# Gate weights loaded together, x copied out of PSUM before it is split, and a weight subtraction moved to VectorE

## The chip, the cores and the metric

The kernel runs on one core of one Trainium2 chip. The metric is the device time of one execution in microseconds (us); lower is better. The time before is a median of 3 runs.

## What is computed

One encoder layer over 1024 tokens of width 1024, all in float32:

```python
xn = rms_norm(x, norm_g)
qa, ka, va, za, qb, kb, vb, zb = split(xn @ w_in)     # eight blocks of 512 columns
ya = diff_attention(rms_norm(qa), rms_norm(ka), va, lam, t5_bias)   # 4 heads, two softmax maps each
ya = rms_norm(ya, subln_g) * (1 - lam_init) * silu(za)
yb = neighbourhood_attention(rms_norm(qb), rms_norm(kb), vb, na_rpb) * silu(zb)  # 8 heads, 8 x 16 window
x = x + concat(ya, yb) @ w_out
x = x + sigmoid(x @ w_ple_gate) * (p @ w_ple_proj)
```

## The kernel before

Every float32 operand of a product is split into a rounded high part and the remaining low part. A product is three matmuls (high by high, high by low, low by high). ScalarE (ACT) makes the high part with a copy, VectorE (DVE) the low part with a subtraction.

**The stages.** Up to 25 us the first row tiles of `x` are normalised, transposed and split. From 25 to about 303 us the input projection runs. It takes the six column blocks kb, vb, qb, qa, ka, va as three pairs, and works each pair with seven products of 512 x 512 quarters (P1 to P7, Winograd's scheme) in place of eight. P2 of all three pairs comes first, then P1, P6, P7, P4, P5, P3 of each pair. Each product is two steps on TensorE (PE) of 24 matmuls (L232 to L234), some 5.5 us each, 42 steps (`NS`) in all. Step h = 0 works the row tiles 0 and 1 of its quarter, step h = 1 the tiles 2 and 3. Neighbourhood attention follows to about 480 us, then differential attention to about 720 us, then the output projection and the last gate.

**The order.** Each engine executes its instructions in the order in which the program is written. Between the matmuls of step i the program places `hooks[i]`: pieces of other work with a number of their own. The tiles come from pools whose buffers go round: the weights `wraw` (L97 loads, 128x512) and many small tiles share pool b2 (11 buffers), wider tiles use b4 (8), and 4 PSUM buffers serve transposes and small products. All ordinary loads and stores leave by one queue of SyncE (SP), in program order. Two engines that read the same PSUM tile are put in order one after the other.

**x_trans(t)** (L360): PE transposes a row tile into two PSUM tiles `xtp` (L368). For tiles 0 to 3 `split` makes the quarters A11 and A12 (high `xh`, L357 on ACT; low `xl`, L358 on DVE), and ACT copies both PSUM tiles in float32 to `xf` (L373), which later sums need. `x_trans(2)`, a small product (`ple_mm(4)`, L312, result `pp` at L314), `x_trans(3)` and `x_norm(4)` stand in this order in the hook of step 0, between its two halves.

**The weights of P6** (`RIGHT`): its right factor is a sum of three quarters. `w_load` loads two raw quarters r and o per 128 rows. `w_sum1` subtracts r - o on GpSimd (POOL, L179). `w_sum2` adds the result to the quarter b11 that P1 left (L191, DVE), one chunk of 128x512 at a time. Two chunks are treated per step, for pair 0 in the iterations i = 5 and i = 6. In the same iterations `x_splits` gives POOL one more sum, `xsum` (L395), and DVE the low parts of S1, S2 and S3.

**The gates.** The columns zb and za (512 each) are taken as eight gate columns of 128. `z_load` loads a column's raw weights `zraw`, `z_split` makes the halves `zw` (L555 on ACT, L558 on DVE), and the product `zps` (L580 to L582) fills PE's gaps in neighbourhood attention. For the za columns the finished halves `zth` are stored to DRAM (`uad`). With `small=True` a column comes in two loads of 256 KB into b2 tiles, without it in one load of 512 KB into a b4 tile. The first column is loaded small in the hook of step NS - 4, the second whole in that of step NS - 1.

**Neighbourhood attention** works 32 units. A unit has scores on PE (`nsp`, L645), bias and maximum on DVE (L660), exponentials on ACT (L665), the division on DVE (L671, L673), transposes on PE (`ntp`, L683), their copy on ACT (`PT`, L685), the product with the values on PE (`npv`, L698) and the gate on DVE (`nay`, L708). Its operands K, Q, R and Vw come over the SP queue.

Of the kernel before, what the change touches and what calls it, by code (L numbers as in the profile page):

```python
# [11 lines left out]
OP = mybir.AluOpType  # L12
# [3 lines left out]
P = 128  # L16
# [8 lines left out]
COL = dict(qa=0, ka=512, va=1024, za=1536, qb=2048, kb=2560, vb=3072, zb=3584)  # L25
# [15 lines left out]
def layer_kernel(ctx, tc, x, p, ngr, w_in, w_out, gains, lamv, t5p, rpbp, w_gate, w_ple,  # L41
# [13 lines left out]
    def T8(shape, dt=F32, n="t8"):  # L55
        return sb.tile(shape, dt, name=nm(n), tag="b8", bufs=16)

    def T4(shape, dt=F32, n="t4"):
        return sb.tile(shape, dt, name=nm(n), tag="b4", bufs=8)

    def TA(shape, dt=F32, n="ta"):
        return sb.tile(shape, dt, name=nm(n), tag="a4", bufs=6)

    def T2(shape, dt=F32, n="t2"):
        return sb.tile(shape, dt, name=nm(n), tag="b2", bufs=NB2)
# [17 lines left out]
    def PS(shape, n="ps"):  # L83
        return psp.tile(shape, F32, name=nm(n), tag="ps", bufs=4)
# [11 lines left out]
    def ld(o, i):  # L96
        return nc.sync.dma_start(raw(o), raw(i))  # L97

    def st(o, i):
        return nc.sync.dma_start(raw(o), raw(i))  # L100
# [7 lines left out]
    V = nc.vector  # L108
# [48 lines left out]
    raws = {}  # L157
# [14 lines left out]
    def w_sum1(j):  # L172

        if j >= len(chunks):
            return
        pi, n, k = chunks[j]
        if n == "P6":
            r, o = raws[j]
            G.tensor_tensor(r, r, o, op=OP.subtract)  # L179
        elif n == "P4":  # L180
            r = raws[j][0]
            G.tensor_tensor(r, r, tk["t2", k], op=OP.subtract)

    def w_sum2(j):

        if j >= len(chunks):
            return
        pi, n, k = chunks[j]
        if n == "P6":
            r, t = raws[j][0], tk["b11", k]  # L190
            V.tensor_tensor(t, t, r, op=OP.add)  # L191
            tk["t3", k], tk["t2", k] = r, t
            raws[j] = t
        elif n == "P7":
            raws[j] = tk.pop(("t3", k))
        elif n == "P5":
            r, t = raws[j][0], tk.pop(("t2", k))
            V.tensor_tensor(t, r, t, op=OP.subtract)
            tk["b22", k] = r
            raws[j] = t  # L200
        elif n == "P3":
            raws[j] = tk.pop(("b22", k))
        else:
            raws[j] = raws[j][0]
# [150 lines left out]
    def split(n, ts, src, low):  # L355
        h, l = XA[n]
        act(h[:, :, ts], src, AF.Copy)  # L357
        low.tensor_tensor(l[:, :, ts], src, h.bitcast(F32)[:, :, ts], op=OP.subtract)  # L358

    def x_trans(t):  # L360
        hat = xhats.pop(t)
        u = t % 4
        ts = slice(u * P, u * P + P)
        pt = [PS([P, 4, P], "xtp") for _ in range(2)]
        for b in range(2):
            for k in range(4):
                kc = 4 * b + k
                nc.tensor.transpose(pt[b][:, k], hat[:, kc * P:(kc + 1) * P], idn)  # L368
        if t < 4:
            split("A11", ts, pt[0], V)  # L370
            split("A12", ts, pt[1], V)
            for b in range(2):
                act(xf[b][:, u], pt[b], AF.Copy)  # L373
            return
        s, d = xsum[0][:, u], xsum[1][:, u]
        a21 = TA([P, 4, P], n="a21s")
        act(a21, pt[0], AF.Copy)
        pst.append(lambda: st(a21d[:, :, ts], a21))
        V.tensor_tensor(s, pt[1], a21, op=OP.add)
        split("A22", ts, pt[1], V)  # L380
        V.tensor_tensor(d, xf[0][:, u], pt[0], op=OP.subtract)
        split("S1", ts, s, V)
        V.tensor_tensor(s, s, xf[0][:, u], op=OP.subtract)

    xsum = []
    xf = []
# [14 lines left out]
    def x_reload():  # L401
        r = T8([P, 4, 512], n="a21r")
        ld(r, a21d)
        XA["a21r"] = r

    def x_resplit():
        r = XA["a21r"]
        XA["A21"] = (T8([P, 4, 512], F32R, n="xh"), T8([P, 4, 512], F32R, n="xl"))
        h, l = XA["A21"]
        for k in range(2):  # L410
            ks = slice(2 * k, 2 * k + 2)
            act(h[:, ks], r[:, ks], AF.Copy)
            zl.append(lambda ks=ks: V.tensor_tensor(l[:, ks], r[:, ks], h.bitcast(F32)[:, ks], op=OP.subtract))
# [124 lines left out]
    def z_load(col, small=False):  # L538
        src = w_in[:, col:col + P].rearrange("(k q) d -> q k d", q=P)
        if small:  # L540
            r = [T2([P, 4, P], n="zraw") for _ in range(2)]
            for i in range(2):
                ld(r[i], src[:, 4 * i:4 * i + 4])
            zraw[col] = lambda a, b: r[a // 4][:, a % 4:(b - 1) % 4 + 1]
            return
        r = T4([P, 8, P], n="zraw")
        ld(r, src)
        zraw[col] = lambda a, b: r[:, a:b]

    def z_split(col, k0=0, k1=8):  # L550
        r = zraw[col]
        if k0 == 0:
            zw[col] = T8([P, 2, 8, P], F32R, n="zw")
        w = zw[col]
        act(w[:, 0, k0:k1], r(k0, k1), AF.Copy)  # L555

        def low():
            V.tensor_tensor(w[:, 1, k0:k1], r(k0, k1), w.bitcast(F32)[:, 0, k0:k1], op=OP.subtract)  # L558

        zl.append(low)  # L560
# [4 lines left out]
    def z_low():  # L565
        while zl:
            zl.pop(0)()
# [37 lines left out]
    def load_k(pr):  # L605
        k1 = T8([P, 2, S], F32R, n="K1")
        h, l = qkd["kb"]
        for (dst, s) in ((k1[0:64], h), (k1[64:128], l), (K2[pr % 2][0:64], h)):
            ld(dst, s[pr].rearrange("(h d) s -> d h s", h=2))
        kb[pr] = k1  # L610

    def load_q(pr, R):
        q1 = T4([P, 2, 512], F32R, n="Q1")
        h, l = qkd["qb"]
        for (dst, s) in ((q1[0:64], h), (q1[64:128], h), (Q2[R][0:64], l)):
            ld(dst, s[pr, :, R * 512:(R + 1) * 512].rearrange("(h d) s -> d h s", h=2))
        qb[pr, R] = q1

    def load_r(pr):
        r = []  # L620
        for h in range(2):
            t = TA([P, 752], n="R")
            ld(t, ap_of(rpbp, (2 * pr + h) * 23 * 48 + 1, [[48, 8], [1, 16], [1, 752]]))
            r.append(t)
        Rt[pr] = r

    def load_v(pr, R, j):
        w = WID[j]
        v = T15([P, 3, P], n="Vw")
        for m in range(3):  # L630
            r0 = 4 * R + 4 * m
            ld(v[0:4 * w, m], ap_of(vbd, (r0 * 64 + COL0[j]) * 512 + pr * P, [[64 * 512, 4], [512, w], [1, P]]))
        Vw[pr, R, j] = v
# [94 lines left out]
    def na_consts_q():  # L728
        for R in range(2):
            q = T4([P, 2, 512], F32R, n="Q2")  # L730
            for h in range(2):
                cast(q[64:128, h], onehot[:, R * 512:(R + 1) * 512])
            Q2.append(q)

    def load_r0():
        t = T8([P, 2, 752], n="R0")
        Rt[0] = [t[:, h] for h in range(2)]
        for h in range(2):
            ld(t[:, h], ap_of(rpbp, h * 23 * 48 + 1, [[48, 8], [1, 16], [1, 752]]))
# [90 lines left out]
    def pre(i):  # L830
        if i >= len(units):
            return
        pr, R, j = units[i]
        if j == 0:
            if R == 0:
                load_q(pr, 1)
            elif pr + 1 < 4:
                load_q(pr + 1, 0)
        if (R, j) == (0, 2) and pr + 1 < 4:
            load_k(pr + 1)  # L840
        if (R, j) == (1, 2) and pr + 1 < 4:
            load_r(pr + 1)
        if i + 2 < len(units):
            load_v(*units[i + 2])
# [22 lines left out]
    for j in range(6):  # L867
        w_sum2(j)
# [6 lines left out]
    ple_t(3)  # L875
    w_split(1)
    x_trans(0)
    ple_mm(2)
    ple_st()
# [54 lines left out]
    def s7():  # L934
# [3 lines left out]
    NS = len(steps)  # L938
# [8 lines left out]
        31: lambda: u_load(31),  # L947
        NS - 7: lambda: (na_consts_k(), load_k(0)),
        NS - 5: lambda: (load_r0(), x_reload()),
        NS - 4: lambda: z_load(COL["zb"], True),  # L950
        NS - 2: lambda: (na_consts_q(), load_q(0, 0), load_v(0, 0, 0), load_v(0, 0, 1), z_split(COL["zb"], 0, 4),
                         z_split(COL["zb"], 4, 8), z_low()),
        NS - 1: lambda: (pre(0), x_resplit(), z_load(COL["zb"] + P)),
        NS: na_consts_k,
    }
    lam_in = []
    normed = []
    for i in range(len(steps) + 2):
        w_sum1(LA - 2 + 2 * i)
        w_sum1(LA - 1 + 2 * i)  # L960
        if i < len(steps):
            step_mm(i, 0, 2)
# [4 lines left out]
        if got:  # L967
            n, t0, c = got
            if n[0] == "v":
                v_evac(n, t0, c)  # L970
            else:
                normed.append((n, t0, c, qk_norm1(c)[1]))
        w_sum2(LA - 2 + 2 * i)
        w_sum2(LA - 1 + 2 * i)
        w_load(LA + 2 * i)
        w_split(4 + 2 * i)
# [480 lines left out]
```

## Time and profile before

| | |
|---|---|
| median of 3 runs | 836.67 us (835.38 to 838.21) |
| the profiled execution | 838.91 us, of which 837.1 us span |
| mean granted TensorE clock | 0.978 |
| busy | PE 94%, PEld 78%, DVE 61%, ACT 52%, POOL 32% |

The span is what the trace covers; 1.81 us lie around it. PE is TensorE's matmuls and PEld its weight loads, which run beside them. A name such as `xl<-xtp` reads "tile xl written from tile xtp". "Idle before" is the time in which the engine did nothing ahead of that instruction, followed by what ended it.

### The profile page before, as it was taken

The numbers are of one execution on the slowest core, as the hardware profiler recorded it, in microseconds if no ns is written. First come the engines' busy times: TensorE is split into PE (matmuls) and PEld (weight loads), VectorE is DVE, ScalarE is ACT, GpSimd is POOL, SyncE is SP. The second block draws the span as 40 slices with busy tenths as digits, with TensorE's granted clock in tenths as the row PEclk, the third lists the DMA queues.
The fourth block names the chain that finished last, engine by engine and source line by source line (L and its number), as shares of the span: only waits on it lengthen the run. The fifth ranks groups of instructions, "written<-read, shape, count | busy, mean of one in ns | idle before, by whom it ended". The sixth has DMA issues, their size and how long they took to land.

```text
span 837.1 us, 12190 instructions
## 1 busy us (share of the span) xinstructions
PE 783.7 (94%) x4242; PEld 649.8 (78%) x4242; DVE 511.8 (61%) x986; ACT 437.6 (52%) x814; POOL 266.2 (32%) x267
## 2 busy tenths in 40 slices
PE   7899799999989994998979998999999999999997
PEld 6678588888878883776767776888888877888886
DVE  4557795685997662653635658777777752732332
ACT  5665355255435532554545569889888861411120
POOL 1003443261565400110101124677776761200000
PEclk9999899999999997999999999999999999999999
DMA  8655461945788999576666768757686437223222
GB/s 330 272 175 172 170 186 59 325 128 132 173 280 241 217 298 235 140 178 180 200 168 183 175 206 225 216 154 209 163 236 174 144 124 268 85 76 101 83 94 88
DMA packets 118525, 151.94 MB, mean 181 GB/s; under 512 B 23832, under 2 KB 76728, under 8 KB 118336
## 3 DMA queue, kind: packets, MB, share of 16 engines
q1 hardware_dynamic: 116672, 145.39, 59.0%
q0 software_dynamic: 1792, 5.77, 2.2%
q8 instruction: 34, 0.56, 0.3%
q14 instruction: 27, 0.22, 0.1%
HBM read 104.96 MB, written 46.17 MB: 181 GB/s over the span
## 4 chain that ended last, share of the span: by engine, by line
PE 71%; DVE 8%; DMA 7%; ACT 5%; issue 4%; SPq 2%; POOL 2%; ACTq 0%; DVEq 0%; POOLq 0%
PE ips L232 7%; PE ips L234 7%; PE ips L233 7%; PE dsp L1064 6%; PE gps L1259 3%; PE gps L1257 3%; PE gps L1258 3%; PE dtp L1106 3%; DMA uad<-zth 3%; PE ntp L683 3%; PE pps L312 2%; PE zps L580 2%; PE zps L582 2%; PE zps L581 2%; DMA Vw<-vb 2%
## 5 line engine op out<-in xcount | busy, mean ns | idle before, releaser
L232 PE MATMUL ips<-w,xh 128*128 128x512 f32 x336 | 135.0, 402 | 5.6 <-DVE C L258 4.1
L234 PE MATMUL ips<-w,xl 128*128 128x512 f32 x336 | 132.5, 394 | 0.0
L233 PE MATMUL ips<-w,xh 128*128 128x512 f32 x336 | 132.3, 394 | 0.0
L1089 POOL TENSOR_TENSOR s<-s,s 128x1024 f32<-128x1024 f32 x32 | 77.0, 2408 | 56.9 <-ACT s L1088 52.3
L431 POOL TENSOR_TENSOR qrs<-qms,nhalf 128x16 f32<-128x16 f32 x16 | 51.7, 3233 | 91.5 <-DVE qms L429 91.5
L1074 DVE CUSTOM_DVE_ANT_0 s<-dsp,T 128x1024 f32<-128x1024 f32 x64 | 77.7, 1215 | 2.5 <-PE dsp L1064 2.5
L232 PEld LDWEIGHTS ips<-w,xh 128*128 128x128 f32 x336 | 64.2, 191 | 19.3 <-issue 4.8
L1076 ACT ACTIVATE s<-s,dm 128x1024 f32<-128x1024 f32 x64 | 73.4, 1146 | 4.6 <-DVE dm L1074 4.5
L234 PEld LDWEIGHTS ips<-w,xl 128*128 128x128 f32 x336 | 63.9, 190 | 13.9
L233 PEld LDWEIGHTS ips<-w,xh 128*128 128x128 f32 x336 | 64.2, 191 | 13.1 <-DVE w L216 0.3
L1064 PE MATMUL dsp<-K,Q 128*128 128x512 f32 x256 | 69.7, 394 | 4.9 <-DVE dm L1074 4.3
L1113 DVE TENSOR_TENSOR aTl<-dtp,aTh 128x512 fp32r<-128x512 f32 x64 | 44.2, 691 | 46.9 <-ACT aTh L1107 46.9
L714 POOL TENSOR_TENSOR yb<-nay,yb 128x128 fp32r<-128x128 f32 x32 | 16.2, 508 | 174.5 <-ACT yb L713 174.5
L216 DVE TENSOR_TENSOR w<-wraw,w 128x512 fp32r<-128x512 f32 x84 | 62.2, 778 | 5.9 <-ACT w L215 5.4
L1064 PEld LDWEIGHTS dsp<-K,Q 128*128 128x128 f32 x256 | 45.9, 189 | 14.6 <-issue 3.0
L685 ACT ACTIVATE PT<-ntp 96x768 f32<-96x768 f32 (+1 forms) x32 | 25.9, 810 | 59.2 <-PE ntp L683 59.2
L580 PE MATMUL zps<-xh,zw 128*128 128x512 f32 x128 | 54.3, 424 | 0.0
L582 PE MATMUL zps<-xh,zw 128*128 128x512 f32 x128 | 51.1, 399 | 0.0
L581 PE MATMUL zps<-xl,zw 128*128 128x512 f32 x128 | 51.0, 398 | 0.0
L215 ACT ACTIVATE w<-wraw 128x512 fp32r<-128x512 f32 x84 | 48.4, 625 | 4.7 <-DVE wraw L191 4.5
L1257 PE MATMUL gps<-wgh,x1h 128*128 128x512 f32 x128 | 50.5, 395 | 0.0
L1107 ACT ACTIVATE aTh<-dtp 128x512 fp32r<-128x512 f32 x64 | 38.0, 593 | 23.1 <-PE dtp L1106 23.1
(174 smaller groups left out, 1823.2 us busy)
## 6 DMA issues: line engine op xcount, KB each, us to landing
wraw<-in_w_in_dram SPq DMA_DIRECT2D x72, 256.0 KB
x<-in_x_dram SPq DMA_DIRECT2D x8, 512.0 KB
ppd<-pp SPq DMA_DIRECT2D x8, 512.0 KB
K<-kbh SPq DMA_DIRECT2D x8, 512.0 KB
Q<-qbh SPq DMA_DIRECT2D x16, 256.0 KB
Q<-qah SPq DMA_DIRECT2D x16, 256.0 KB
Q<-qal SPq DMA_DIRECT2D x16, 256.0 KB
wor<-in_w_out_dram SPq DMA_DIRECT2D x8, 512.0 KB
```

The lines of the kernel that those rows point to most:

```text
L216: V.tensor_tensor(w[:, 1], r, w.bitcast(F32)[:, 0], op=OP.subtract)
L232: mm(ps, lh[:, k, a:a + P], w[:, 0], start=(new and k == 0), stop=False, skip_group_check=cont)
L233: mm(ps, lh[:, k, a:a + P], w[:, 1], start=False, stop=False, skip_group_check=cont)
L234: mm(ps, ll[:, k, a:a + P], w[:, 0], start=False, stop=(k == 3), skip_group_check=cont)
L580: mm(ps, w[:, 0, kc], xh(kc, a, b), start=(kc == 0), stop=False)
L581: mm(ps, w[:, 0, kc], xl(kc, a, b), start=False, stop=False)
L582: mm(ps, w[:, 1, kc], xh(kc, a, b), start=False, stop=(kc == 7))
L1064: mm(ps[:, cs], q[g][:, m, u * P:(u + 1) * P], k[:, cs], start=(g == 0), stop=(g == 1))
L1074: V.tensor_tensor_reduce(out=s, in0=ps, in1=back(Td[h][:, :], 1919 - (896 - P * qt), [[-1, S]]), scale=-1.0, scalar=BIG, op0=OP.add, op1=O ...
L1076: act(s, s, AF.Exp, bias=mx, scale=-1.0, accum_out=z[:, m:m + 1])
L1089: G.tensor_tensor(s1, s1, s2, op=OP.add)
L1257: mm(ps, h[:, k], wh, start=(k == 0), stop=False)
```

## The change

Three edits. In `x_trans` the float32 copies `xf` of tiles 0 to 3 come first, and the splits of A11 and A12 read `xf` in SBUF instead of the PSUM tiles. For pair 0 the four subtractions of P6's right factor move from POOL (`w_sum1`) to DVE (`w_sum2`), ahead of the additions. And the second gate column is loaded right behind the first, in the same form: two loads of 256 KB in the hook of step NS - 4, in place of one of 512 KB in that of step NS - 1. PE's instructions keep their order.

```diff
@@ w_sum1
-        if n == "P6":
+        if n == "P6" and pi:
             r, o = raws[j]
             G.tensor_tensor(r, r, o, op=OP.subtract)
@@ w_sum2
         if n == "P6":
             r, t = raws[j][0], tk["b11", k]
+            if not pi:
+                V.tensor_tensor(r, r, raws[j][1], op=OP.subtract)
             V.tensor_tensor(t, t, r, op=OP.add)
@@ x_trans
         if t < 4:
-            split("A11", ts, pt[0], V)
-            split("A12", ts, pt[1], V)
             for b in range(2):
                 act(xf[b][:, u], pt[b], AF.Copy)
+            split("A11", ts, xf[0][:, u], V)
+            split("A12", ts, xf[1][:, u], V)
             return
@@ hooks
-        NS - 4: lambda: z_load(COL["zb"], True),
+        NS - 4: lambda: (z_load(COL["zb"], True), z_load(COL["zb"] + P, True)),
...
-        NS - 1: lambda: (pre(0), x_resplit(), z_load(COL["zb"] + P)),
+        NS - 1: lambda: (pre(0), x_resplit()),
```

In the changed kernel most lines stand two further down (L357 becomes L359, L191 becomes L193).

On ACT, the rows of x_trans(0), the first of the four such places (x_trans(2) reads the same with other numbers). Before:

```order
L215 ACTIVATE w_250<-wraw_122 128x512
L357 ACTIVATE xh_175<-xtp_253 128x4x128
L357 ACTIVATE xh_177<-xtp_254 128x4x128
L373 ACTIVATE xf_181<-xtp_253 128x512
L373 ACTIVATE xf_182<-xtp_254 128x512
L314 ACTIVATE pp_269<-pps_270 128x512
```

and after:

```order
L217 ACTIVATE w_250<-wraw_122 128x512
L373 ACTIVATE xf_181<-xtp_253 128x512
L373 ACTIVATE xf_182<-xtp_254 128x512
L359 ACTIVATE xh_175<-xf_181 128x4x128
L359 ACTIVATE xh_177<-xf_182 128x4x128
L316 ACTIVATE pp_269<-pps_270 128x512
```

The two copies have moved ahead of the two high parts, and the high parts no longer read PSUM.

On DVE, the rows of iteration i = 5, from the last low parts of `x_splits` to the low parts of the next weights. Before:

```order
L358 TENSOR_TENSOR xl_676<-xsum_564,xh_675 128x4x128
L358 TENSOR_TENSOR xl_678<-xd_565,xh_677 128x4x128
L191 TENSOR_TENSOR wraw_550<-wraw_550,wraw_730 128x512
L191 TENSOR_TENSOR wraw_555<-wraw_555,wraw_737 128x512
L216 TENSOR_TENSOR w_806<-wraw_637,w_806 128x512
```

and after:

```order
L360 TENSOR_TENSOR xl_676<-xsum_564,xh_675 128x4x128
L360 TENSOR_TENSOR xl_678<-xd_565,xh_677 128x4x128
L192 TENSOR_TENSOR wraw_730<-wraw_730,wraw_732 128x512
L193 TENSOR_TENSOR wraw_550<-wraw_550,wraw_730 128x512
L192 TENSOR_TENSOR wraw_737<-wraw_737,wraw_739 128x512
L193 TENSOR_TENSOR wraw_555<-wraw_555,wraw_737 128x512
L218 TENSOR_TENSOR w_806<-wraw_637,w_806 128x512
```

The subtractions `wraw_730` and `wraw_737`, which POOL made, now stand on DVE, each ahead of its addition; iteration i = 6 has the same difference.

On SP, the end of the projection's loads (R is a bias table of neighbourhood attention, a21r a quarter of x read back, kah and kal the stores of ka). Before:

```order
L97 DMA R_507_2543<-in_rpb_dram 128x1x752 x2
L97 DMA a21r_2546<-a_23_100 128x2048
L97 DMA zraw_2593<-in_w_in_dram 128x4x128
L97 DMA zraw_2594<-in_w_in_dram 128x4x128
L100 DMA kah_103<-sth_2609 128x4x256
```

and after:

```order
L97 DMA R_507_2543<-in_rpb_dram 128x1x752 x2
L97 DMA a21r_2546<-a_23_100 128x2048
L97 DMA zraw_2593<-in_w_in_dram 128x4x128
L97 DMA zraw_2594<-in_w_in_dram 128x4x128
L97 DMA zraw_2597<-in_w_in_dram 128x4x128
L97 DMA zraw_2598<-in_w_in_dram 128x4x128
L100 DMA kah_103<-sth_2613 128x4x256
```

Two loads are new ahead of the store `kah`; the 512 KB load that stood some 17 rows further down, behind the first loads of Q and Vw, is gone.

## Rows read from the trace of the kernel before

**Rows 1.** The page's 40 slices of 20.9 us: busy tenths, and granted clock.

```profile
PE   7899799999989994998979998999999999999997
PEclk9999899999999997999999999999999999999999
```

**Rows 2.** Timeline of PE: start, duration, engine, line, operation, count [idle before <-releaser].

```profile
35.89 1.72 PE L368 MATMUL xtp<-idn,xhat 128*128 128x128 f32 x8 [3.18 <-ACT xf L373]
37.83 0.63 PE L233 MATMUL ips<-w,xh 128*128 128x512 f32 x1
...
39.91 0.39 PE L232 MATMUL ips<-w,xh 128*128 128x512 f32 x1
...
44.95 0.74 PE L312 MATMUL pps<-wph,ph 128*128 128x512 f32 x2 [0.53 <-ACT ph L298]
```

**Rows 3.** Timeline of ACT around x_trans(2) and x_trans(3).

```profile
31.97 1.07 ACT L357 ACTIVATE xh<-xtp 128x512 fp32r<-128x512 f32 x2
35.24 1.20 ACT L373 ACTIVATE xf<-xtp 128x512 f32<-128x512 f32 x2 [2.20 <-DVE xl L358]
36.33 1.08 ACT L314 ACTIVATE pp<-pps 128x512 f32<-128x512 f32 x2
```

**Rows 4.** Timeline of DVE over the same stretch.

```profile
34.52 1.28 DVE L358 TENSOR_TENSOR xl<-xtp,xh 128x512 fp32r<-128x512 f32 x2
37.94 1.29 DVE L358 TENSOR_TENSOR xl<-xtp,xh 128x512 fp32r<-128x512 f32 x2 [2.13 <-ACT xh L357]
```

**Rows 5.** Timeline of POOL in iteration 5.

```profile
79.02 1.68 POOL L395 TENSOR_TENSOR xsum<-xf,xsum 128x512 f32<-128x512 f32 x1 [5.71 <-DVE xl L358]
80.66 2.55 POOL L179 TENSOR_TENSOR wraw<-wraw,wraw 128x512 f32<-128x512 f32 x2
```

**Rows 6.** Timeline of DVE in iterations 5 and 6.

```profile
81.99 2.36 DVE L191 TENSOR_TENSOR wraw<-wraw,wraw 128x512 f32<-128x512 f32 x2 [2.44 <-POOL wraw L179]
...
93.08 2.35 DVE L191 TENSOR_TENSOR wraw<-wraw,wraw 128x512 f32<-128x512 f32 x2 [2.44 <-POOL wraw L179]
```

**Rows 7.** Timeline of PE over the same stretch.

```profile
89.31 0.50 PE L232 MATMUL ips<-w,xh 128*128 128x512 f32 x1 [1.51 <-ACT C L262]
...
94.68 0.39 PE L234 MATMUL ips<-w,xl 128*128 128x512 f32 x1
99.12 0.77 PE L232 MATMUL ips<-w,xh 128*128 128x512 f32 x1 [4.06 <-DVE C L258]
...
104.38 0.54 PE L232 MATMUL ips<-w,xh 128*128 128x512 f32 x1
```

**Rows 8.** Groups by line: count | busy us, mean ns of one | idle before.

```profile
L191 DVE TENSOR_TENSOR wraw<-wraw,wraw 128x512 f32<-128x512 f32 x12 | 11.0, 956 | 4.9 <-POOL wraw L179 4.9
L198 DVE TENSOR_TENSOR wraw<-wraw,wraw 128x512 f32<-128x512 f32 x12 | 8.0, 685 | 7.6 <-DMA wraw<-in_w_in_dram 7.6
```

**Rows 9.** Timelines of PE and ACT where the second gate column is first used.

```profile
326.48 1.51 PE L683 MATMUL ntp<-idn,nas 128*96 128x128 f32 x6 [11.55 <-DVE nas L673]
...
324.16 0.63 ACT L555 ACTIVATE zw<-zraw 128x512 fp32r<-128x512 f32 x1 [12.61 <-DMA zraw<-in_w_in_dram]
```

**Rows 10.** Timeline of SP's DMA issues.

```profile
272.77 1.46 SPq L97 DMA_DIRECT2D zraw<-in_w_in_dram  x2
289.09 0.37 SPq L100 DMA_DIRECT2D kah<-sth  x1
...
316.92 0.42 SPq L97 DMA_DIRECT2D zraw<-in_w_in_dram  x1
...
372.39 0.34 SPq L100 DMA_DIRECT2D uad<-zth  x1
373.26 8.75 SPq L97 DMA_DIRECT2D Vw<-vb  x3
```

**Rows 11.** Timelines of ACT and DVE where they wait for a store of that queue.

```profile
384.10 0.60 ACT L586 ACTIVATE zth<-zps 128x512 f32<-128x512 f32 x1 [6.48 <-DMA uad<-zth]
...
435.43 0.29 DVE L708 TENSOR_TENSOR nay<-npv,zth 128x128 f32<-128x128 f32 x1 [5.47 <-DMA uad<-zth]
```

## The prediction

> **What bounds the kernel now.** I read the page's slices first [rows 1]. PE is at nine tenths or more nearly everywhere, so the time is TensorE's work plus the places where it stops. Three of these belong to the three edits: the second slice, the fifth, and the sixteenth, where PE drops to four tenths and the clock to seven. I then looked at PE's timeline in each for its idle time and for what ended it, and followed the named releaser on its own engine, back to the instruction that the edit touches.
>
> At 35.89 PE waits 3.18 us for ACT's copy `xf` [rows 2]; that copy had waited 2.20 for DVE's low part [rows 3, 4]. At 99.12 PE waits 4.06 us for DVE's sum `C` [rows 7]; ahead of it DVE had waited twice 2.44 for POOL's subtractions [rows 6]. At 326.48 PE waits 11.55 us; the chain runs back over DVE and ACT to ACT's `zw`, which waited 12.61 for the raw weights of the second gate column [rows 9].
>
> After long stops the matmuls are slower for a while: 0.63 us instead of 0.39 until 39.9 [rows 2], as at the lower level of TensorE's clock, 1.2 in place of 2.4 GHz. From 37.83 to 39.91 five starts took 2.08, 0.42 each. The step at 89.31, behind a stop of 1.51, made 23 starts in 5.37, 0.23 each [rows 7]: there the clock stayed up. So a stop of 3.18 costs more than itself: of the 4.02 us from 35.89 to 39.91 some 1.8 are the clock's (4.02 x (1 - 0.23/0.42)).
>
> **Edit 1, x copied first: 3.9 us.** Nothing is added or removed; ACT runs the same four operations in another order. ACT comes to x_trans(2) at 31.97 either way. Then both copies (1.20 the pair, [rows 3]) are done at 33.1, and the PSUM tiles are free without DVE: PE, whose last matmuls ended at 32.7 (35.89 less 3.18), transposes tile 3 from about 33.2 and stops for 0.5. A stop of that size, less than the 1.51 above, should leave the clock up.
>
> The second half of step 0 follows at 34.0 and takes 12 x 0.23 = 2.75, to 36.8. What is late next is the low part of tile 3, which step 1 needs with its sixth matmul, at 37.9. ACT runs on from 33.1: high parts 1.07, `pp` 1.08, copies 1.20, high parts 1.07, to 37.5; DVE's low parts end near 38.2 against 39.2 before [rows 4]. PE waits 0.3. Step 1's first half ends near 39.8 instead of 44.0, and with the waits for ACT behind it the small product that began at 44.95 [rows 2] begins at about 41.05: **3.9 us**.
>
> Bounds: if the clock still falls, the 1.8 are lost again, which leaves 2.1. If nothing waits behind it, 4.2. The operations themselves change no price that I can see: the four reads of SBUF in place of PSUM stay within the same 0.6 us of ACT. I take 3.9, since every step of the chain is an existing row.
>
> **Edit 2, subtractions on DVE: 2.5 us.** POOL loses 2.55 us of work in each iteration [rows 5], DVE gains two operations. DVE is free at 79.55 (81.99 less 2.44), but POOL's `xsum` runs until 80.70 [rows 5]. What two engines cost each other shows in the additions: beside POOL's subtraction the pair took 2.36 [rows 6] and the mean of twelve is 956 ns, while the like operation L198, without POOL beside it, takes 685 [rows 8].
>
> Taking from this pair that an operation begun beside POOL ends about 0.55 behind POOL's, the first subtraction ends at 81.25, and three more at 0.61 apiece end at 83.1. The pair of additions ended at 84.35. That is 1.23 earlier; iteration 6, with the same 2.44 and the same `xsum` on POOL, repeats it, and DVE hardly waits in between. DVE's `C` comes 2.46 earlier, PE's step at about 96.65 instead of 99.12.
>
> PE itself arrives 1.23 earlier, because its 1.51 at 89.31 also hangs on DVE, by way of ACT; so 2.8 of the 4.06 stay. Whether the clock falls after 2.8 no row shows; 3.18 did it and 1.51 did not. I take the nearer, 3.18: the clock falls and the gain is **2.5**. If it stays up, the twelve starts from 99.12 to 104.38, 5.26 us, take 2.8, so 2.5 less. I count 1.1 of it, since the transposes that follow wait for the norm that POOL and DVE make of the same `C`: 3.6. Bounds of the shared time: with no hold by POOL four operations from 79.55 at 0.61 end at 82.0, 2.4 per iteration earlier; with each of the four held to 1.2 (half of 2.36) they end at 84.3, no gain.
>
> The Trainium skill, GPSIMD Engine Reference, section Key points, says that GpSimd shares its SBUF interfaces with VectorE and contends with DVE instructions that have two SBUF inputs. It speaks against this edit, which puts four such instructions on DVE just when `xsum` runs. By it the gain is the 2.5 of the held case, and without it nearer 4.8. The 956 against 685 agrees with the rule.
>
> **Edit 3, the second gate column loaded early: 0.8 us.** The load was issued at 316.92 and ACT had it at 324.16 [rows 9, 10]. Now it leaves behind the first column's pair of 272.77. SP has nothing else until the store at 289.09 [rows 10], so nothing is queued that the two loads could hold up. The direct effect is large: 11.55 of idling goes, and a slow stretch like that of [rows 2], some 1.8: 13.4 in all.
>
> But neighbourhood attention is fed by one queue. The three Vw issues from 373.26 take 8.75 us [rows 10], where one takes about half a us when nothing holds it. SP is not waiting for the engines there, but for earlier transfers to land. ACT at 384.10 waits 6.48 for a store of that queue, and DVE at 435.43 waits 5.47 for another [rows 11]. In the changed order the same tile waits for the same store, and that store stands behind the same transfers. PE would run ahead by 13 us from 315 on and give it back by 384.
>
> What remains is what the queue itself gains. One load of 512 KB leaves the crowded stretch. A pair of 256 KB takes SP 1.46 to issue, and the load's share of the stream is of that order, an estimate: 0 to 1.5 us. I take the middle, **0.8**. What the gain depends on is that the projection's 6.4 us reach the queue: its stores and loads from 289 on wait for results of that stage, so it begins earlier by as much.
>
> **The sum.** 3.9 + 2.5 + 0.8 = 7.2 us. The profiled execution took 838.91, so 831.7; it stands 2.24 above the median of 836.67, and by the median the time is **829.5 us**. The three ranges give 827.4 (4.2 + 3.6 + 1.5 = 9.3 saved) to 834.6 (2.1 + 0 + 0).
>
> **The rivals.** *The run-ahead of edit 3 is kept.* The waits of [rows 11] would go too if the queue could send earlier once its tiles come free earlier. Then 13.4 comes in place of 0.8, and the time is 816.9. For it: PE stops nowhere as long. Against it: the 8.75 us of issue, and two later waits for the same queue. In between, PE could keep a part. Chance 0.15.
>
> *The gain of the projection is given back.* If the stretch from 40 to 100 us is paced by loads of weights rather than by the engines, edit 1 only lengthens the waits of edit 2: edit 1 gives nothing, and with the held case on DVE only the 0.8 remains, 835.9; with half of edit 2 it is 834.6. For it: the weights of each product are loaded a few steps ahead, in the same queue. Against it: the releasers named there are engines, not DMAs [rows 2 to 7]. Chance 0.16, of which 0.05 is still faster than 0.3%.
>
> *The early loads hold up the queue.* They now stand ahead of the stores of ka and of the first loads for attention. If these land later by as long as the load took, 7.2 us (316.92 to 324.16), PE stops there for it, restarts at the low clock for 1.8, and nothing behind makes it good: 836.67 - 6.4 + 9.0 = 839.3, and 841.8 if edit 2 gives nothing either. It decides once delay and restart together pass the 6.4. Against it: SP is idle from 274.2 to 289.09, long enough for the whole transfer. Chance 0.07.
>
> **How the numbers follow.** The forecast has the remaining 0.62. A measurement of this kernel can tell about 0.3%, 2.5 us, from no change, so faster is below 834.2: 0.62 + 0.15 + 0.05 = 0.82. Within: 0.11. Slower, above 839.2 (the third rival, which lies about there or beyond): 0.07. For 8 in 10 the forecast's own range, 827.4 to 834.6, is carried up to the second rival's 836 and down to where nearly all of the run-ahead is kept, 818.
>
> **What would show it.** In the profile of the changed kernel: the transposes at about 33.2 with 0.5 of idle before them, and 0.39 matmuls behind; no wait of DVE for POOL near 80 and 90, and PE's wait for `C` near 2.8 instead of 4.06; no 11.55 before `ntp`, and in its place longer waits before 384 that end on the store `uad` or on loads of the SP queue. The forecast is wrong if those waits are short (then the time is near 817), or if PE waits as long for DMAs between 40 and 100 us as it did for DVE.

## The result, and the profile after

The changed kernel took 827.88 us (median of 4 runs, 825.45 to 831.1) where the kernel before took 836.23 beside it: a ratio of 0.9899 (95% interval 0.9859 to 0.9939). Measured again with the experiments it took 826.96 against 838.17, 0.9868 (0.9849 to 0.9887). The forecast was 829.5, with a range of 818 to 836. The profiled execution took 825.45 us, the shortest of the four, of which 823.7 are the span.

The slices of the page of the changed kernel (20.6 us each), to set against [rows 1]:

```profile
PE   7999899999989999797989988999999999999997
PEclk9999999999999999999989999999999999999999
```

The hole of the sixteenth slice is gone, and the clock's seven with it. Two shallower ones have come behind it, in the seventeenth and nineteenth slice (330 to 350 and 371 to 391 us).

The first edit, in PE's, ACT's and DVE's timeline of the changed kernel (start, duration, engine, line, operation, count [idle before <-releaser]), to set against [rows 2 to 4]:

```profile
32.39 1.06 PE L370 MATMUL xtp<-idn,xhat 128*128 128x128 f32 x8 [0.58 <-DVE xhat L354]
39.63 0.74 PE L314 MATMUL pps<-wph,ph 128*128 128x512 f32 x2 [0.47 <-ACT ph L300]
40.90 0.73 PE L314 MATMUL pps<-wph,pl 128*128 128x512 f32 x2 [0.53 <-DVE pl L301]
...
31.05 1.08 ACT L373 ACTIVATE xf<-xtp 128x512 f32<-128x512 f32 x2
32.00 1.16 ACT L359 ACTIVATE xh<-xf 128x512 fp32r<-128x512 f32 x2
...
35.66 1.29 DVE L360 TENSOR_TENSOR xl<-xf,xh 128x512 fp32r<-128x512 f32 x2 [0.77 <-ACT xh L359]
```

The 3.18 us are 0.58, and the transposes take 1.06 instead of 1.72, so the clock is up. What PE waits for is no longer ACT but DVE's normalised row `xhat`. A short wait is new at 40.90, for DVE's low part `pl`; the kernel before has none there.

The second edit, in the timelines of DVE, POOL and PE of the changed kernel, to set against [rows 5 to 7]:

```profile
74.95 1.78 DVE L192 TENSOR_TENSOR wraw<-wraw,wraw 128x512 f32<-128x512 f32 x1
76.77 0.69 DVE L193 TENSOR_TENSOR wraw<-wraw,wraw 128x512 f32<-128x512 f32 x1
...
74.51 1.68 POOL L397 TENSOR_TENSOR xsum<-xf,xsum 128x512 f32<-128x512 f32 x1 [5.72 <-DVE xl L360]
...
83.75 0.50 PE L234 MATMUL ips<-w,xh 128*128 128x512 f32 x1 [0.61 <-ACT C L264]
...
92.53 0.47 PE L234 MATMUL ips<-w,xh 128*128 128x512 f32 x1 [3.03 <-DVE C L260]
...
94.09 0.63 PE L234 MATMUL ips<-w,xh 128*128 128x512 f32 x1
```

The first subtraction ends at 76.73, 0.54 behind the end of POOL's `xsum` (76.19); the operations after it take 0.69. PE's wait is 3.03 instead of 4.06, and the one ahead of it 0.61 instead of 1.51. The first five matmuls take 0.39 to 0.47, the sixth 0.54, and from 94.09 to 97.1 they take 0.63.

The third edit, in the timelines of PE, DVE and ACT of the changed kernel, to set against [rows 9 and 11]:

```profile
307.61 0.82 PE L685 MATMUL ntp<-idn,nas 128*96 128x128 f32 x6
...
348.69 1.65 PE L647 MATMUL nsp<-K,Q 128*128 128x384 f32 x4 [4.35 <-DVE nam L662]
...
346.20 0.46 DVE L662 CUSTOM_DVE_ANT_1 nas<-nsp,R 128x288 f32<-128x288 f32 x1 [6.05 <-DMA R<-in_rpb_dram]
...
371.80 0.60 ACT L588 ACTIVATE zth<-zps 128x512 f32<-128x512 f32 x1 [5.74 <-DMA uad<-zth]
```

PE comes to `ntp` 18.87 us earlier than before (326.48) and no longer stops there. The lead is given back in the main at the loads of R, where the kernel before does not wait: counted from SP's store `kah` (below), ACT's copies `PT`, one per unit, stand 11.1 us earlier than before at the eighth unit and 4.5 at the ninth. At the store `uad` the kernel before waits as well (6.48, [rows 11]), and there the lead does not shrink (4.4 and 5.1 on either side). What is left, the experiments take apart.

### The profile page after: what moved, and what is told of

Its sections match the earlier page's. It is cut to its first block, busy times and chain, and to the rows that moved or that the text cites. A ratio compares the mean times of both kernels' runs of the same rounds, so it can differ in the third digit from the quotient of the medians.

```text
span 823.7 us, 12188 instructions
## 1 busy us (share of the span) xinstructions
PE 781.7 (95%) x4242; PEld 647.9 (79%) x4242; DVE 514.6 (62%) x990; ACT 437.2 (53%) x814; POOL 261.3 (32%) x263
## 4 chain that ended last, share of the span: by engine, by line
PE 65%; DMA 11%; DVE 11%; ACT 5%; issue 3%; SPq 3%; POOL 2%; DVEq 0%; ACTq 0%; POOLq 0%
PE dsp L1066 6%; PE ips L234 6%; PE ips L236 6%; PE ips L235 6%; PE gps L1261 4%; PE gps L1259 4%; PE gps L1260 4%; DMA Vw<-vb 3%; PE dtp L1108 3%; SPq L97 2%; PE ntp L685 2%; DMA wraw<-in_w_in_dram 2%; PE dpv L1135 2%; PE zps L582 2%; PE zps L584 2%
```

## The experiments

A median says little about where time goes, and one trace has its own chance. So I read two landmarks in each trace: SP's first store `kah` behind the gate loads (289.09 before, [rows 10]), which closes the part that the first two edits touch, and PE's first `dsp` that waits for DVE's `dm`, 1.41 us in every trace, where differential attention begins (498.51 before). Between them lies neighbourhood attention with its crowded queue. The table holds the start times read from the timelines, and the difference:

| kernel | edits 1, 2, 3 | kah | dsp | between | ratio to before (interval) |
|---|---|---|---|---|---|
| before | | 289.09 | 498.51 | 209.42 | |
| before_again | | 288.08 | 496.74 | 208.66 | 1.0001 (0.9989 to 1.0013) |
| only_copies | 1 | 284.66 | 492.78 | 208.12 | 0.9981 (0.9966 to 0.9997) |
| only_sums | 2 | 285.95 | 496.62 | 210.67 | 0.9981 (0.9962 to 0.9999) |
| no_gate | 1, 2 | 282.22 | 490.31 | 208.09 | 0.9945 (0.9931 to 0.9959) |
| no_gate_again | 1, 2 | 282.12 | 492.61 | 210.49 | 0.9941 (0.9920 to 0.9962) |
| only_gate | 3 | 288.87 | 494.06 | 205.19 | 0.9973 (0.9956 to 0.9991) |
| after | 1, 2, 3 | 281.93 | 485.91 | 203.98 | 0.9899 (0.9859 to 0.9939) |
| after_again | 1, 2, 3 | 283.62 | 488.31 | 204.69 | 0.9868 (0.9849 to 0.9887) |
| gate_dummy | 1, 2, 3 + a load | 283.27 | 493.15 | 209.88 | 0.9916 (0.9895 to 0.9937) |
| sums_no_pool | 1, 2, 3 | 282.87 | 488.03 | 205.16 | 0.9868 (0.9849 to 0.9886) |
| early_r_uad | 1, 2, 3 | 282.50 | 485.91 | 203.41 | 0.9863 (0.9838 to 0.9888) |
| gate_third4 | 1, 2, 3 | 282.35 | 489.62 | 207.27 | 0.9913 (0.9895 to 0.9932) |
| gate_pool | 1, 2, 3 | 282.55 | 495.15 | 212.60 | 0.9980 (0.9962 to 0.9998) |

**before_again.** The kernel before, unchanged.

> The kernel before, for a second trace of it. If the first profiled execution of 838.91 us was a slow one, this one is at 836 to 838 and shows where two executions of one program differ; the stops of 3.18, 4.06 and 11.55 us should be there again, within 0.5 us. Its ratio to itself should hold 1.

It has a median of 837.63. PE's timeline of this second execution:

```profile
35.42 1.97 PE L368 MATMUL xtp<-idn,xhat 128*128 128x128 f32 x8 [3.18 <-ACT xf L373]
...
98.38 0.76 PE L232 MATMUL ips<-w,xh 128*128 128x512 f32 x1 [4.09 <-DVE C L258]
...
324.53 1.51 PE L683 MATMUL ntp<-idn,nas 128*96 128x128 f32 x6 [10.59 <-DVE nas L673]
```

The two stops of the engines repeat to 0.03 us; the one for a transfer differs by 0.96. The first trace was about 1 us late at `kah`, so I count the first part against 288.59, the mean of the two.

**The edits one by one, and the first two together.** `only_copies` (also `no_gate`):

```diff
-            split("A11", ts, pt[0], V)
-            split("A12", ts, pt[1], V)
             for b in range(2):
                 act(xf[b][:, u], pt[b], AF.Copy)
+            split("A11", ts, xf[0][:, u], V)
+            split("A12", ts, xf[1][:, u], V)
```

> Only the first edit: in x_trans the float32 copies come ahead of the splits. By the forecast this is 3.9 us less than before (2.1 to 4.2), with the transposes of tile 3 at about 33 us and PE's 3.18 us of idling ahead of them down to some 0.5; the profile of the changed kernel, set against that of before instruction by instruction, gives 4.5 at 60 us. The rival, that the time before 100 us is paced by loads and the gain goes into the later wait for C, gives 0 to 1 us less.

`only_sums` (also `no_gate`):

```diff
-        if n == "P6":
+        if n == "P6" and pi:
...
+            if not pi:
+                V.tensor_tensor(r, r, raws[j][1], op=OP.subtract)
```

> Only the second edit: the four subtractions of pair 0's P6 on DVE. By the forecast 2.5 us less than before (0 to 3.6), with PE's wait for C at step 8 near 2.8 us in place of 4.06. The changed kernel's trace gives 2.8. The rival, that DVE is held by POOL for all four operations, gives no gain and the wait of 4.06 stays.

`only_gate`:

```diff
-        NS - 4: lambda: z_load(COL["zb"], True),
+        NS - 4: lambda: (z_load(COL["zb"], True), z_load(COL["zb"] + P, True)),
...
-        NS - 1: lambda: (pre(0), x_resplit(), z_load(COL["zb"] + P)),
+        NS - 1: lambda: (pre(0), x_resplit()),
```

> Only the third edit: the second gate column loaded with the first. By the forecast 0.8 us less than before (0 to 1.5), since PE's 13.4 us of run-ahead are given back at the stores of the SP queue by about 384 us. The rival, to which the changed kernel's trace points (12.6 us ahead behind 480 us, of which 7.2 were there before 300 us), is that some 5.4 us are kept, because SP had waited 4.9 us for PE to release a tile (from 373.26 us) and that wait goes with PE's lead.

`no_gate` has the first two diffs.

> The first two edits without the third. If the edits add up, 6.4 us less than before by the forecast and 7.2 by the changed kernel's trace, and the idling of 11.55 us ahead of the transposes ntp stays, some 7 us earlier. What the changed kernel gains beyond this one is then the third edit's: 0.8 by the forecast, 5.4 by the rival. If the two give less than 4 us, the waits behind take a part back.

and measured once more:

> The first two edits once more, beside the others of this set. If the first measurement (0.9945 of before) holds, the third edit is worth some 4 to 6 us behind them (the changed kernel had 0.9899 and 0.9868). If it comes out near 0.992, the third edit is worth 2 to 4.

The stops of edits 1 and 2, in PE's timelines of only_copies, only_sums and no_gate, in this order:

```profile
33.13 1.06 PE L368 MATMUL xtp<-idn,xhat 128*128 128x128 f32 x8 [0.59 <-DVE xhat L352]
```

```profile
96.61 0.47 PE L234 MATMUL ips<-w,xh 128*128 128x512 f32 x1 [3.04 <-DVE C L260]
```

```profile
92.86 0.77 PE L234 MATMUL ips<-w,xh 128*128 128x512 f32 x1 [3.03 <-DVE C L260]
...
319.30 1.52 PE L685 MATMUL ntp<-idn,nas 128*96 128x128 f32 x6 [11.23 <-DVE nas L675]
```

At `kah` the copies alone are 3.9 us ahead of 288.59, the sums 2.6, both 6.4 and 6.5. Each of the two gains about what its step said, alone or together; with one trace of each single edit, and 1.0 between the two traces of before, that holds to about 0.5 us. The third leaves `kah` where it was and takes its time between the landmarks: 205.19 alone, 203.98 and 204.69 with the others, where the six traces without it have 208.09 to 210.67. The means are 204.6 and 209.2, so 4.6 us.

By the medians each edit alone is worth less than its trace shows: 1.6, 1.6 and 2.3 us (ratios times 837) against 3.9, 2.6 and 4.6. Together they come to what the traces add up to: 8.4 and 11.2 against 11.0. The stretch between the landmarks varies by 2.6 us among traces without edit 3, and I have one or two executions of each. A part is lost behind `dsp`: from there to the end of the span only_copies took 339.4 us and only_gate 340.1, where the two traces of before took 338.6 and 337.7; but that stretch, too, varies by 2.5 us among the traces of all kernels. Where the single edits lose the rest is not settled.

**gate_dummy.**

```diff
-        NS - 1: lambda: (pre(0), x_resplit()),
+        NS - 1: lambda: (pre(0), x_resplit(), z_again()),
...
+    def z_again():
+        c = COL["zb"] + P
+        ld(T4([P, 8, P], n="zagain"), w_in[:, c:c + P].rearrange("(k q) d -> q k d", q=P))
```

> The changed kernel with the second column's 512 KB loaded once more at the place where it stood before, into a tile that nobody reads; what is computed stays the same. If the third edit's lasting gain is that the queue has one load less in its crowded stretch, it is lost: 1 to 2 us slower than the changed kernel. If it comes from PE releasing its tiles earlier, the time stays within 0.5 us of the changed kernel's.

It took 830.63 us, 3.7 more than after_again beside it. The queue, ACT and DVE of gate_dummy:

```profile
310.62 0.83 SPq L97 DMA_DIRECT2D zagain<-in_w_in_dram  x1
...
315.96 0.55 SPq L97 DMA_DIRECT2D zraw<-in_w_in_dram  x1
...
377.04 0.60 ACT L588 ACTIVATE zth<-zps 128x512 f32<-128x512 f32 x1 [7.49 <-DMA uad<-zth]
...
349.20 0.46 DVE L662 CUSTOM_DVE_ANT_1 nas<-nsp,R 128x288 f32<-128x288 f32 x1 [6.27 <-DMA R<-in_rpb_dram]
...
428.65 0.29 DVE L710 TENSOR_TENSOR nay<-npv,zth 128x128 f32<-128x128 f32 x1 [5.52 <-DMA uad<-zth]
```

and the same three waits, ACT's and DVE's, in after_again:

```profile
374.25 0.60 ACT L588 ACTIVATE zth<-zps 128x512 f32<-128x512 f32 x1 [6.98 <-DMA uad<-zth]
...
347.01 0.46 DVE L662 CUSTOM_DVE_ANT_1 nas<-nsp,R 128x288 f32<-128x288 f32 x1 [5.03 <-DMA R<-in_rpb_dram]
...
424.81 0.29 DVE L710 TENSOR_TENSOR nay<-npv,zth 128x128 f32<-128x128 f32 x1 [4.07 <-DMA uad<-zth]
```

PE has the same lead here (`ntp` at 308.96), and between the landmarks it loses all of it: 209.88. The next `zraw` is issued at 315.96; after_again, 0.35 behind at `kah`, issues it at 314.15. So the load costs the queue 2.2 us at once, and the stretch 5.2. The cost grows where an engine waits for this queue: counted from `kah`, the wait for R ends 2.5 us later than in after_again, the first wait for `uad` 3.1 and the second 4.2 later, while between these waits the copies `PT` keep their distance within half a us. The extra load also takes a buffer of b4, but it is not buffers that SP lacks: from 310 to 355 us it waited 1.1 us in all for engines, and 2.5 in after_again. The gain of the third edit is the load that left the stretch, and not PE's lead, nor the tiles that it releases earlier.

**early_r_uad.**

```diff
-        if (R, j) == (1, 2) and pr + 1 < 4:
+        if (R, j) == (1, 0) and pr + 1 < 4:
             load_r(pr + 1)
...
-                    st(uad[(col - COL["za"]) // P][:, hf * 512:hf * 512 + 512], th)
+                    stp(uad[(col - COL["za"]) // P][:, hf * 512:hf * 512 + 512], th)
```

> The changed kernel with the bias tables R asked for two units earlier and the stores uad on POOL's queue in place of SP's. In the changed kernel PE's lead of 20 us falls to 11.6 at two waits, DVE for R (6.05 us at 346) and ACT for uad (5.74 at 372). If the order in the one queue is what takes the lead back, both waits shrink below 2 us and the time falls by 3 to 7. If the transfers as a whole are what binds, other loads are late in their place and the time stays within 1 us.

It took 826.87 us, the same as after_again. DVE's and PE's timelines of early_r_uad:

```profile
342.24 0.46 DVE L662 CUSTOM_DVE_ANT_1 nas<-nsp,R 128x288 f32<-128x288 f32 x1 [0.99 <-DMA R<-in_rpb_dram]
...
344.97 0.44 PE L700 MATMUL npv<-PT,Vw 128*64 128x128 f32 x4 [2.54 <-DMA Vw<-vb]
...
429.14 0.52 PE L700 MATMUL npv<-PT,Vw 128*64 128x128 f32 x4 [3.03 <-DMA Vw<-vb]
```

The wait for R shrank from 6.05 to 0.99 and the ones for `uad` are gone, but the values Vw, which stood behind, are late in their place. In this variant it is the transfers as a whole that set the pace, not which of them stands first.

**gate_third4.** The third gate column early too.

```diff
-        NS - 4: lambda: (z_load(COL["zb"], True), z_load(COL["zb"] + P, True)),
+        NS - 4: lambda: (z_load(COL["zb"], True), z_load(COL["zb"] + P, True), z_load(COL["za"])),
...
-            if i + 2 < len(zseq):
+            if 0 < i < len(zseq) - 2:
```

> The changed kernel with the third gate column's load (512 KB) also taken out of the attention stage, to step NS - 4 behind the other two. The load that was put back cost 3.7 us. If a transfer taken out of the crowded stretch from 300 to 460 us is what pays, this gives another 2 to 4 us: 823 to 825 where the changed kernel has 827. If the stretch before 300 us is as full, the stores and loads that it delays there cost as much: no change, or slower.

It took 830.23 us, 0.9913: slower than the changed kernel's 0.9868 in the neighbouring set, though not to be told from its first 0.9899. In the trace the stretch between the landmarks took 207.27, against 203.98 and 204.69. SP's and DVE's timelines of gate_third4:

```profile
265.77 16.48 SPq L97 DMA_DIRECT2D zraw<-in_w_in_dram  x5
282.35 1.38 SPq L100 DMA_DIRECT2D kah<-sth  x1
...
288.57 1.41 DVE L459 SCALAR_TENSOR_TENSOR stl<-qtp,gk,sth 128x512 fp32r<-128x512 f32 x2 [0.95 <-DMA kah<-sth]
```

In the changed kernel the four gate loads take SP from 265.61 until 279.15 and the store at 281.93 finds it free. The gap is that narrow because the third of the four had to wait for its tile, as the queue's own waits of the changed kernel show for 265 to 278 us (waited for: us in total, times, longest):

```profile
SPq L97 <- DVE C L437: 10.0, 1, 10.0
```

A fifth load fills the gap: the store takes 1.38 to issue instead of 0.37, DVE waits for it, and the first Q load leaves 12.5 us behind the store instead of 11.2 (294.88 and 293.15). Room for one such load was there, not for two.

**gate_pool.** The gate columns that stay in the attention stage go over POOL's queue.

```diff
         r = T4([P, 8, P], n="zraw")
-        ld(r, src)
+        nc.gpsimd.dma_start(r, src)
```

> The changed kernel with the gate columns' loads on POOL's queue instead of SP's; the bytes stay the same. If SP's limit of transfers in flight is what binds, six loads leave it and 3 us or more are gained. If the transfers themselves bind, the time stays within 1 us; if POOL's issue is late for its own work, it is slower.

It took 835.81 us, slower than the changed kernel by about 1.1% of the time before. POOL's and PE's timelines of gate_pool:

```profile
295.43 0.95 POOL L549 DMA_DIRECT2D zraw<-in_w_in_dram  x1 [3.23 <-PE ips L236]
299.49 0.90 POOL L549 DMA_DIRECT2D zraw<-in_w_in_dram  x1 [3.11 <-ACT xh L414]
...
306.91 0.64 PE L647 MATMUL nsp<-K,Q 128*128 128x288 f32 x3 [2.20 <-DMA Q<-qbl]
```

A queue of their own lets these loads leave as soon as their tile is free, ahead of the Q that the first scores need, and PE stops for Q. The same bytes, asked for earlier, push the urgent ones back. Whether fewer loads in SP's queue would gain something if none of them left earlier, this run does not tell.

**sums_no_pool.**

```diff
-        G.tensor_tensor(s, xf[1][:, t % 4], s, op=OP.subtract)
+        V.tensor_tensor(s, xf[1][:, t % 4], s, op=OP.subtract)
```

> The changed kernel with the four sums xsum of x_splits on DVE instead of POOL, so that no POOL operation runs beside the moved subtractions. If the 1.78 us of the first subtraction is POOL's hold, it falls to 0.69, each iteration ends some 0.5 us earlier (1.1 less the 0.6 of the sum itself), and PE's 3.03 us of waiting at step 8 falls to about 2; 0.5 to 1.5 us less than the changed kernel, more if the clock then stays up. If something else holds it, a load or a semaphore, it stays at 1.78 and DVE ends 1.2 later: about 1 us slower.

It took 826.86 us against 826.96 of after_again; the 0.5 to 1.5 us that were expected did not come. Timelines of DVE and PE of sums_no_pool:

```profile
75.64 0.68 DVE L397 TENSOR_TENSOR xsum<-xf,xsum 128x512 f32<-128x512 f32 x1
76.25 0.68 DVE L192 TENSOR_TENSOR wraw<-wraw,wraw 128x512 f32<-128x512 f32 x1
76.96 0.69 DVE L193 TENSOR_TENSOR wraw<-wraw,wraw 128x512 f32<-128x512 f32 x1
...
92.82 0.77 PE L234 MATMUL ips<-w,xh 128*128 128x512 f32 x1 [3.06 <-DVE C L260]
```

The subtraction falls from 1.78 to 0.68, so it was POOL that held it: 1.1 us, twice. Counted from the transposes (33.57, and 32.39 in the changed kernel), PE's step begins after 59.25 instead of 60.14, 0.9 earlier. The stop ahead of it stays, since PE comes earlier too. Here the matmuls are at 0.77 and 0.63 at once, and twelve of them take 5.26 us, where the changed kernel's first trace had five fast ones and needed 4.12; that alone is more than the 0.9. after_again, the same kernel, needs 5.26 too. How little such a gain is worth at this step, early_r_uad shows, where the clock did not fall (last section). None of the variants is measurably faster than the changed kernel.

**after_again.** The changed kernel, for the comparisons above.

> The changed kernel itself, once more, beside the others of this set. The single edits gave 1.9, 1.7 and 0.8 us, 4.4 in all, the first two together 4.7, and all three 8.4. If the third edit is worth more behind the first two, the time stays near 828. If the four runs of the first measurement were short by chance, it comes to about 831.4 (832.2 of the two edits less 0.8).

## Why the prediction was right, and where it was not

**Edit 1, forecast 3.9, measured 3.9 at `kah`.** The transposes came with 0.58 of idling ahead of them instead of the forecast 0.5. The number is in part luck. The trace ran some 0.9 us early here, so counted from the end of PE's work ahead of the stop (32.71 before, 31.81 now): the low parts of tile 3 ended after 5.14 (forecast 5.5), PE did not wait 0.3 for them, and the small product began after 7.82 instead of 12.24. That is 4.4, beyond the stated bound of 4.2. Right behind, PE waits for DVE's `pl` (0.53 at 40.90), which the forecast did not have, and the gain is 3.7. Another releaser was missed ahead of the transposes: PE waited for `xhat`, which DVE finished while ACT copied.

**Edit 2, forecast 2.5, measured 2.6 at `kah`.** The held case was the right one: the subtraction ended 0.54 behind POOL's sum where 0.55 was assumed, and the wait is 3.03 where 2.8 was expected. The four operations took 3.84 us (74.95 to 78.79) instead of the forecast 3.55, and PE's two waits shrank by 1.9 in all, not 2.5; the rest came behind that step and was not followed. The choice on the clock held in the changed kernel: it fell. In early_r_uad it did not, and that gained nothing, where the forecast would have counted 1.1. That the hold is POOL's is shown by sums_no_pool: with POOL out of the way the same operation takes 0.68. With that the trace agrees with the rule of the Trainium skill (GPSIMD Engine Reference, Key points) that the forecast weighed.

**Edit 3, forecast 0.8 (0 to 1.5), measured 4.6.** This term was mis-sized. Its mechanism held in the main: PE ran ahead at 307.61, gave the lead back to the queue, and kept what the queue gained by having one load less. The place was another: the lead went at the loads of R, by about 355 us, and not at the store `uad`. Nor did the second pair of loads leave right behind the first: SP waited 10.0 us for a tile, and of the idle stretch that the forecast counted on 2.8 us were left. The price of that load was taken from the 1.46 us that SP needs to issue a pair. That is what the issue costs, not what the transfer costs a queue that is behind: 2.2 us at the next issue of the same kind, and 4 to 5 by the end of the stage (3.7 by the medians, 5.2 by the traces of gate_dummy and after_again). It grows at the waits for R and `uad`, as gate_dummy shows. One sentence on the way was wrong too: of the three Vw issues at 373.26, the first did wait for an engine, as the queue's own waits show for 370 to 384 us of the kernel before (waited for: us in total, times, longest):

```profile
SPq L97 <- PE zps L582: 4.9, 1, 4.9
```

That wait was the ground for the rival in only_gate's expectation, that PE's earlier release of tiles pays. gate_dummy has PE's lead and no such gain, so it falls.

**The sum.** The forecast 7.2 was 3.9 + 2.5 + 0.8; the traces give 6.4 at `kah` and 4.6 behind it, 11.0, and the two measurements 8.4 and 11.2. By the medians the first two edits gave less than the forecast 6.4, namely 4.6 and 4.9 (no_gate and no_gate_again), and the third, behind them, 3.9 and 6.1. So the total came out near the forecast partly because two errors had opposite signs. **The rivals.** The run-ahead was not kept: 4.6 of some 13. The projection's gain was not given back before 300 us: it stood at 6.4 at `kah`. The early loads did not hold up the queue, but gate_third4 shows that the margin was one load.

## What to carry to other kernels

Where a stage is fed by one crowded queue, take a transfer out of that stage and put it where the queue rests: that paid 4 to 5 us in the traces here for 512 KB (2.3 to 6.1 by the medians), while moving other transfers forward within the stage made others late, in both variants that tried it. Price such a transfer by what it delays behind it, not by the time of its issue, and look whether the place it goes to still has room for it and a free tile. Where two engines read one PSUM tile, let the copy that frees it come first.

## What had not been expected of the hardware

After stops of 3.03 to 3.06 us at the same step, the clock did three things. It was low from the first matmul (0.77, then 0.63) in no_gate, no_gate_again, sums_no_pool and after_again. It fell after five fast matmuls in the first trace of the changed kernel (granted clock 0.50 from 94.10 to 97.10). And it did not fall at all in early_r_uad (granted clock 1.00 from 92.60 to 95.40), whose edits act only behind 300 us. PE's timeline of early_r_uad:

```profile
92.59 0.47 PE L234 MATMUL ips<-w,xh 128*128 128x512 f32 x1 [3.04 <-DVE C L260]
...
99.28 1.09 PE L446 MATMUL qtp<-idn,C 128*128 128x128 f32 x8 [0.99 <-DVE C L437]
```

Counted from the restart, twelve matmuls took 2.82 us there instead of 4.12. But the transposes `qtp` then wait 0.99 for DVE and begin after 6.69 instead of 7.18, and `kah` comes after 189.91 instead of 189.40: in this trace the faster matmuls were worth nothing at the end of the stage.
